# A two-layer hybrid encoder in one kernel: offsets between moving and next stationary operands changed

## The chip, the cores and the metric

The kernel runs on one core of a Trainium2 chip. The metric is device time in microseconds of one execution; the smaller the better. TensorE (PE) multiplies: each matmul has a stationary operand, loaded first by an instruction of its own (PEld), and a moving operand that streams past it; both lie in SBUF, the sums in PSUM. VectorE (DVE), ScalarE (ACT) and GpSimd (POOL) do the rest, and SyncE (SP) issues most transfers.

## The reference

Two pre-norm layers over 256 tokens of width 2048, each a token mixer with 4 cross-attention heads into 256 memory tokens beside it, an output projection, and a squared-ReLU MLP of width 8192. Layer 0's mixer is a neighbourhood attention with a bias per offset, layer 1's a grouped-query attention with normed heads and rotary positions.

```python
m = rms_norm(mem, mem_norm)
h = x
for i in range(DEPTH):
    n = rms_norm(h, attn_norm[i])
    ...
        z = n @ a_w_in[j]
        q, k, v, qm = jnp.split(z, [MIX_WIDTH, 2 * MIX_WIDTH, 3 * MIX_WIDTH], axis=-1)
        mix = neighbourhood_attention(split_heads(q, N_MIX_HEADS), split_heads(k, N_MIX_HEADS),
                                      split_heads(v, N_MIX_HEADS), a_rpb[j])
    ...
    km, vm = jnp.split(m @ w_mem_kv[i], 2, axis=-1)
    cross = memory_attention(split_heads(qm, N_MEM_HEADS), split_heads(km, N_MEM_HEADS),
                             split_heads(vm, N_MEM_HEADS))
    h = h + jnp.concatenate([mix, cross], axis=-1) @ w_o[i]
    n = rms_norm(h, mlp_norm[i])
    h = h + jnp.square(jax.nn.relu(n @ w_up[i])) @ w_down[i]
return rms_norm(h, final_norm)
```

## The kernel before

Every product is done in three matmuls of type float32r: an operand is split into a high part (ScalarE, L483: the name with `h`, as `hi`, `uh`, `bh`, `th`) and the rest (VectorE, L484: the name with `l`, as `lo`, `ul`, `bl`, `tl`), and high x high, high x low and low x high are summed in PSUM. Weights come from DRAM in chunks of 1 MB and are split half a chunk at a time.

There are two kinds of product. In an S product (`products`, L375, and its matmuls at L387) the weights are stationary and 256 tokens of an activation move, so a matmul has 256 columns; `k` counts the 16 slices (kt) of the inner dimension, and each has three matmuls: high weights with the activation's high part, high weights with its low part, low weights with its high part. In an M product (`m_products`, L355) the activations are stationary and 512 columns of weights move.

The stages in order: memory projections; layer 0's input projections and attention; its output projection; its MLP; the same for layer 1. In an MLP, 64 up chunks (`up_grains`, sum `ps_u`) give 128 features each. The first LEAD = 6 run alone. Then 58 steps follow (`STEPS`), each a part of the down product by Strassen's seven products (sums `p`, L1167 to L1170) around one up chunk: 12 matmuls on `bh`, `bl`; 48 of the up chunk; 9 on `th`, `tl`. That is 116 steps in both layers. The steps go in 8 runs a layer (`RUNS`), and at a run's end the seven sums are taken out of PSUM (`taken`). What Strassen leaves is done plainly (`plain_grains`, operands `h_p`, `l_p`, `uh`, `ul`); the last of these blocks, the closing block, is cut into 512 and twice 256 columns.

The order on each engine is decided by a scheduler when the program is built, from its own model of the times; `pin` and `issue_after` hold single instructions in place. Buffers go round by tag: `uh` and `ul` have two buffers each, so a split into one waits until PE has read its last use.

Tiles are placed in SBUF one behind the other by pool. The attention's pool (`work`) stands on the right side; the MLP's split weights are in `side` and `mlp`. Where an operand begins within 128 bytes is set by constants at the top, in bytes: MOVING_AT (weights that move, in a `uh` or `ul` buffer), LAST_AT (how far one half of the normed activation `hT` is set off in the last kt, class `Shifted`), LAST_COPY_AT (a copy `hT_l` of the last kt's first half, made at L1059 for the lead chunks and handed out by class `Plain`), U_AT and COPY_AT (the copy `u` of an up chunk's first stationary operand, made at L1049).

In an up chunk the last kt's three matmuls are, in order: high weights with the activation's second half, high weights with its first half, low weights with its first half (L381 and L382).

Of the kernel before, what the change touches and what calls it, by code (L numbers as in the profile page):

```python
# [46 lines left out]

MOVING_AT = 160

LAST_AT = 224  # L50

LAST_COPY_AT = 32

U_AT = 96

# [3 lines left out]

LONGER = {"hi": 128, "lo": 128}  # L60

COPY_AT = 384
MASKED = -1e30


# [12 lines left out]
class Work:  # L78


    def __init__(self, kind, src, acts, first, begins, last, start, done):
        self.kind, self.src, self.acts = kind, src, acts
        self.first, self.begins, self.last, self.start, self.done = first, begins, last, start, done
        self.early = self.behind = self.last_block = False


class Shifted:
# [5 lines left out]
    def __getitem__(self, key):  # L93
        _, k, s = key
        at = k * 512 + (s.start or 0)
        if k == KT - 1:

            at = k * 512 + (0 if s.start else SEQ + LAST_AT // 4)
        return self.room[:, at : at + SEQ]


class Plain:


    def __init__(self, shifted, last):
        self.shifted, self.last = shifted, last

    def __getitem__(self, key):
        _, k, s = key
        return self.shifted[key] if s.start or k < KT - 1 else self.last  # L110


class Near:
# [45 lines left out]
def encoder_kernel(ctx: ExitStack, tc: tile.TileContext, t: dict, out: bass.AP):  # L159
# [36 lines left out]

    def open_work():
        at.work = opened("work", side="right", bufs=2)

    open_sums(banks=2)  # L200
    open_ring()
# [173 lines left out]
    def products(ps, acts, k0, nk, hi, lo, keep_order=False, first=None):  # L375

        for j in range(nk):
            k = k0 + j
            s = slice(j * P, (j + 1) * P)
            parts = [(hi, slice(0, SEQ)), (hi, slice(SEQ, 512)), (lo, slice(0, SEQ))]  # L380
            if k == KT - 1:  # L381
                parts[:2] = parts[1::-1]  # L382
            elif j == 0 and isinstance(lo, Entered):
                parts = parts[2:] + parts[:2]
            for n, (x, part) in enumerate(parts):
                x = first if n == j == 0 and first is not None else x[:, s]
                ins = nc.tensor.matmul(ps, x, acts[:, k, part], start=k == n == 0,  # L387
                                       stop=k == KT - 1 and n == 2)
                if keep_order and n == 0:
                    pin(ins)  # L390
# [355 lines left out]
    def km_done(layer, hd):  # L746
        def f(w):
            if layer == 0:
                later((12, 12, 13, 8)[hd], put, w)
            else:  # L750
                put(w)

        def put(w):
            s = summed(w.ps, "km", box["mem_row"])
            if layer == 0:
                if hd == 0:
                    box["km"] = keys("km")
                split(box["km"][:, hd, :SEQ], box["km"][:, hd, SEQ:], s)
            else:
                k = at.work.tile([P, 512], F32R, tag="b_y2", name="km_w")  # L760
                split(k[:, :SEQ], k[:, SEQ:], s)
                nc.sync.dma_start(mem_k[:, hd, :], k.bitcast(F32))
        return f

    def vm_done(layer):
        def f(w):
            if layer == 0:
                box["vm"] = values("values", "vm", 1)
                put_values(box["vm"], w.ps, box["mem_col"])
                return  # L770
            for i in range(NT):
                v = at.work.tile([P, 2, 512], F32R, tag="pT", name="vm_w")
                put_value(v, w.ps[i], box["mem_col"][:, i : i + 1])
                nc.sync.dma_start(mem_v[:, i], v.bitcast(F32))
        return f

    def mem_back():

        box["km"] = keys("km")
        box["vm"] = values("values", "vm", 1)  # L780

        def load():

            with tc.issue_after(box["load"].ins):
                nc.sync.dma_start(box["km"].bitcast(F32), mem_k)
                for i in range(NT):
                    nc.sync.dma_start(box["vm"][:, :, i, :].bitcast(F32), mem_v[:, i])
        later(4, load)
# [231 lines left out]
    def up_grains(layer, m):  # L1020
        own = {}
        lead = m < LEAD

        def load():
            own["raw"] = loaded(t[f"w_up{layer}"][m], "U")

        def prep(hf):

            with tc.issue_after(box["summed"].ins) if m in (1, 2) else nullcontext():
                prepared(hf)  # L1030

        def prepared(hf):
            half = 2 * m + hf
            if lead and (half in (2, 4) or half > 4 and half % 3 == 2):

                if half < 5:
                    room = at.side.tile([P, 2, HALF], F32R, tag="b", bufs=2, name="u_b")
                    own[hf] = room[:, 0], room[:, 1]
                else:
                    s = slice(U_AT // 4, U_AT // 4 + HALF)  # L1040
                    own[hf] = tuple(at.mlp.tile([P, 3 * 512], F32R, tag=x, name=f"u_{x}")[:, s] for x in ("th", "tl"))
                box["splits"].append(split(*own[hf], own["raw"][:, hf * HALF : (hf + 1) * HALF]))
            else:
                own[hf] = half_of_side(own["raw"], hf)
            if not lead and hf == 0:

                room = at.side.tile([P, 256], F32R, tag="junk", bufs=1, name="u_0")
                own["first"] = room[:, COPY_AT // 4 :][:, :P]
                nc.scalar.activation(own["first"], own["raw"][:, :P], AF.Copy)  # L1049

        def run(hf):
            if m == hf == 0:
                closed("cat", "ring")
                at.mlp = opened("mlp")
                box["z"] = [at.mlp.tile([P, 4, 512], F32, tag=f"z{q}", name=f"z{q}") for q in range(2)]
                box["z_set"] = set()

                last = at.mlp.tile([P, 14 * P], F32R, tag="a", bufs=6, name="hT_l")[:, LAST_COPY_AT // 4 :][:, :SEQ]
                nc.scalar.activation(last, box["hT"][:, KT - 1, :SEQ].bitcast(F32), AF.Copy)  # L1059
                box["hT0"] = Plain(box["hT"], last)  # L1060
            if hf == 0:
                if lead:
                    own["ps"] = at.acc.tile([P, 512], F32, tag="acc", name="ps_u")[:, :SEQ]
                else:
                    own["ps"] = sum_of("up")[:, :SEQ]

            with tc.issue_after(box["late"].ins) if m == hf == 0 else nullcontext():
                products(own["ps"], box["hT0" if lead else "hT"], hf * (KT // 2), KT // 2, *own.pop(hf),
                         keep_order=not lead, first=own.pop("first", None))

        def after():
            squared(layer, m, own["ps"])

        soon = (8, 8, 3) if m == 1 else SOONER
        return [Grain(lambda: run(0), None, load, None, lambda: prep(0), soon),
                Grain(lambda: run(1), after, None, None, lambda: prep(1), SOONER)]

# [166 lines left out]
    def plain_grains(layer, nb, at_chunk):  # L1244
# [8 lines left out]

        def prep(c, hf):
            if (at_chunk + c) % 2 == 0:
                own[c, hf] = half_of_side(own[c], hf, MOVING_AT)
            else:
                own[c, hf] = tuple(at.mlp.tile([P, HALF], F32R, tag="bt"[hf] + x, name=f"{x}_p") for x in "hl")
                box["rest"] = split(*own[c, hf], own[c][:, hf * HALF : (hf + 1) * HALF])


# [152 lines left out]
    def rope_tables(name, c, factor=1.0):  # L1414

        cst = box["cst"]
        g = cst[:, c : c + HD]
        cg = at.work.tile([P, NT, HD], F32, tag="cos", bufs=1, name=f"cos_{name}")
        sg = at.work.tile([P, NT, HD], F32, tag="sin", bufs=1, name=f"sin_{name}")
        gs = g.rearrange("p (a b c) -> p a b c", a=2, b=2)  # L1420
        for i in range(NT):
            pin(nc.vector.scalar_tensor_tensor(cg[:, i, :], cst[:, C_COS + i * HD : C_COS + (i + 1) * HD], factor, g,
                                               op0=ALU.mult, op1=ALU.mult))
            s = cst[:, C_SIN + i * HD : C_SIN + (i + 1) * HD].rearrange("p (a b c) -> p a b c", a=2, b=2)
            d = sg[:, i, :].rearrange("p (a b c) -> p a b c", a=2, b=2)
            for b in range(2):
                pin(nc.vector.scalar_tensor_tensor(d[:, :, b, :], s[:, :, b, :], factor, gs[:, :, 1 - b, :],
                                                   op0=ALU.mult, op1=ALU.mult))
        box["rope"] = (cg, sg)
# [288 lines left out]
```

## Time and profile before

| | us |
|---|---|
| median of 3 runs | 2001.03 |
| lowest, highest of them | 1998.95, 2001.11 |
| profiled execution | 1999.8 |
| its span, first to last instruction | 1998.0 |

The mean granted TensorE clock over the span was 0.999 of full speed. The costliest groups of the page, by tile and engine:

| group | count | busy us | mean ns of one |
|---|---|---|---|
| PE L387, up chunks, high weights | 3812 | 663.0 | 276 |
| PE L387, up chunks, low weights | 1960 | 541.3 | 276 |
| ACT L483 `uh` | 262 | 277.7 | 1061 |
| DVE L484 `ul` | 262 | 318.3 | 1219 |
| DVE L484 `bl` | 116 | 265.2 | 2286 |
| DVE L484 `tl` | 116 | 203.5 | 1754 |

How to read the lines below: PE is the matmul, PEld its weight load. In a view of the timeline a line has the start in us from the span's start, the duration in us, the engine, the line, the operation, output<-inputs and shape, with x2 where two like instructions were merged; in brackets stands the engine's idle time before it and what ended that. A group's line ends with the count, busy us and mean ns of one, then the idle time before the group. A line of a stretch has its start and end, its length, and then busy us and count of PE, PEld, DVE, ACT and POOL, the granted clock, the share of DMA and GB/s. A matmul's duration is modelled and longer than the distance to the next one's start.

### The profile page before, as it was taken

Reading aid. Unit: us, or ns where it says so; the run is one execution under the profiler, and the core shown is the slowest. Engines: PE = TensorE matmul, PEld = TensorE weight load, DVE = VectorE, ACT = ScalarE, POOL = GpSimd, SP = SyncE. Lnnn points to the kernel's source line nnn. Section 1 sums busy time; section 2 is a strip of 40 time slices with the busy share of each in tenths; the row PEclk is TensorE's granted clock in tenths of the full one; section 3 lists DMA queues with packets and bytes.
Section 4 is the critical chain, followed back from the end, with each engine's and each line's share of the span. In section 5 each row is a group of like instructions: output and inputs, shape, how many; then the busy total and the mean of one; then the engine's idle time right before and its main releaser. Section 6 shows DMA issues by size and latency. Waiting matters only on the chain.

```text
span 1998.0 us, 32972 instructions
## 1 busy us (share of the span) xinstructions
PE 1985.7 (99%) x12872; PEld 1802.5 (90%) x12872; DVE 1722.1 (86%) x2164; ACT 1277.5 (64%) x1747; POOL 122.8 (6%) x169
## 2 busy tenths in 40 slices
PE   9999999999999999999999999999999999999998
PEld 8999999899999999999998888899999999999987
DVE  6777767589899999999999868779998999999997
ACT  6655555577676666666666666667666666666664
POOL 0000000000000000000000010000000000000000
PEclk9999999999999999999999999999999999999999
DMA  7856555757777777777667765557777777777763
GB/s 286 312 195 208 200 191 184 272 170 252 229 229 233 229 221 241 232 238 237 205 218 239 241 213 189 191 178 238 237 233 231 226 229 234 227 236 234 227 222 128
DMA packets 106862, 446.17 MB, mean 223 GB/s; under 512 B 18257, under 2 KB 39761, under 8 KB 59217
## 3 DMA queue, kind: packets, MB, share of 16 engines
q1 hardware_dynamic: 89712, 413.12, 58.6%
q0 software_dynamic: 16704, 30.42, 9.0%
q8 instruction: 101, 1.65, 0.3%
q10 hardware_dynamic: 288, 0.52, 0.1%
q14 instruction: 57, 0.46, 0.1%
HBM read 397.78 MB, written 4.19 MB: 201 GB/s over the span
## 4 chain that ended last, share of the span: by engine, by line
PE 95%; DVE 2%; DMA 1%; issue 1%; ACT 0%; SPq 0%; DVEq 0%; POOLq 0%; POOL 0%; ACTq 0%
PE ps_u L387 34%; PE ps_s L387 10%; PE p L1169 9%; PE p L1170 9%; PE p L1167 9%; PE ps_m L367 7%; PE ps_m L364 7%; PE ps_m L368 7%; DMA b<-b 0%; DVE lo L484 0%; DMA pT_t<-sc_t 0%; DMA first<-in_mem_rest 0%; DVE bl L484 0%; PE av L672 0%; PE av L673 0%
## 5 line engine op out<-in xcount | busy, mean ns | idle before, releaser
L387 PE MATMUL ps_u<-hT,uh 128*128 128x256 f32 x3812 | 663.0, 276 | 0.0
L387 PEld LDWEIGHTS ps_u<-hT,uh 128*128 128x128 f32 x3812 | 578.6, 188 | 5.5
L387 PE MATMUL ps_u<-hT,ul 128*128 128x256 f32 x1960 | 541.3, 276 | 0.0
L483 ACT ACTIVATE uh<-raw_U 128x1024 fp32r<-128x1024 f32 x262 | 277.7, 1061 | 234.3 <-PE ps_u L387 221.3
L387 PEld LDWEIGHTS ps_u<-hT,ul 128*128 128x128 f32 x1960 | 367.9, 188 | 0.0
L484 DVE TENSOR_TENSOR lo<-raw,hi 128x1024 fp32r<-128x1024 f32 (+1 forms) x215 | 254.7, 1191 | 110.0 <-ACT hi L483 108.9
L483 ACT ACTIVATE hi<-raw 128x1024 fp32r<-128x1024 f32 (+1 forms) x215 | 221.6, 1037 | 181.0 <-PE ps_m L368 93.2
L484 DVE TENSOR_TENSOR ul<-raw_U,uh 128x1024 fp32r<-128x1024 f32 x262 | 318.3, 1219 | 15.7 <-ACT uh L483 15.5
L483 ACT ACTIVATE bh<-b 128x2048 fp32r<-128x2048 f32 x116 | 222.9, 1921 | 104.7 <-PE p L1170 89.3
L484 DVE TENSOR_TENSOR bl<-b,bh 128x2048 fp32r<-128x2048 f32 x116 | 265.2, 2286 | 14.6 <-ACT bh L483 14.5
L484 DVE TENSOR_TENSOR tl<-t,th 128x1536 fp32r<-128x1536 f32 x116 | 203.5, 1754 | 37.7 <-ACT th L483 37.0
L483 ACT ACTIVATE th<-t 128x1536 fp32r<-128x1536 f32 x116 | 172.8, 1490 | 44.4 <-PE p L1170 40.9
L1169 PE MATMUL p<-bl,a_s 128*128 128x512 f32 x464 | 180.9, 390 | 1.8 <-DVE bl L484 1.6
L1170 PE MATMUL p<-bh,a_s 128*128 128x512 f32 x464 | 181.3, 391 | 0.0
L1167 PE MATMUL p<-bh,a_s 128*128 128x512 f32 x464 | 180.6, 389 | 0.0
L1139 POOL DMA_DIRECT2D b<-b x116 | 100.6, 867 | 1148.1 <-DVE t L1138 914.1
L387 PE MATMUL ps_s<-nT,hi 128*128 128x256 f32 x896 | 154.6, 277 | 0.0
L1167 PE MATMUL p<-th,a_s 128*128 128x512 f32 x348 | 136.1, 391 | 0.0
L1169 PE MATMUL p<-tl,a_s 128*128 128x512 f32 x348 | 135.8, 390 | 0.0
L387 PEld LDWEIGHTS ps_s<-nT,hi 128*128 128x128 f32 x896 | 135.3, 188 | 0.2
L1170 PE MATMUL p<-th,a_s 128*128 128x512 f32 x348 | 135.4, 389 | 0.0
L387 PE MATMUL ps_s<-nT,lo 128*128 128x256 f32 x448 | 124.2, 277 | 0.0
(304 smaller groups left out, 3500.1 us busy)
## 6 DMA issues: line engine op xcount, KB each, us to landing
raw_U<-in_w_up SPq DMA_DIRECT2D x128, 1024.0 KB, 4.9
b<-in_w_pair SPq DMA_DIRECT2D x116, 1024.0 KB, 4.9
raw<-in_w_o SPq DMA_DIRECT2D x32, 1024.0 KB, 4.9
b<-b POOLq DMA_DIRECT2D x116, 256.0 KB, 3.3
raw<-in_w_b SPq DMA_DIRECT2D x21, 1024.0 KB, 5.2
raw<-in_w_av SPq DMA_DIRECT2D x12, 1024.0 KB, 5.0
raw<-in_w_aq SPq DMA_DIRECT2D x12, 1024.0 KB, 4.9
raw<-in_w_ak SPq DMA_DIRECT2D x12, 1024.0 KB, 4.9
```

The source lines that it names most:

```text
L364: first = nc.tensor.matmul(ps, ah, hi[:, s], start=st, stop=False)
L367: nc.tensor.matmul(ps, ah, lo[:, s], start=False, stop=False)
L368: final = nc.tensor.matmul(ps, al, hi[:, s], start=False, stop=sp)
L387: ins = nc.tensor.matmul(ps, x, acts[:, k, part], start=k == n == 0, stop=k == KT - 1 and n == 2)
L483: first = nc.scalar.activation(dst_hi, src, AF.Copy)
L484: return first, nc.vector.tensor_tensor(dst_lo, src, dst_hi.bitcast(F32), op=ALU.subtract)
L1139: nc.gpsimd.dma_start(b[:, 3, :], b[:, 1, :], accum_op=ALU.add)
L1167: ins = nc.tensor.matmul(ps, a[:, 0, ai, :], hi[:, s], start=begins, stop=False)
L1169: nc.tensor.matmul(ps, a[:, 0, ai, :], lo[:, s], start=False, stop=False)
L1170: nc.tensor.matmul(ps, a[:, 1, ai, :], hi[:, s], start=False, stop=ends)
```

## The change

Offsets of operands change, by constants, by pads, and by an order:

- LAST_AT goes from 224 to 160, and `Shifted` sets off the second half of the last kt where it set off the first: with `s.start` set the operand lies at SEQ + LAST_AT // 4, else at 0, where before it was the other way round.
- In an up chunk (activations of class `Shifted`) the last kt's matmuls now run low weights first, then high weights with the first half, then high weights with the second half. For the other S products the order stays.
- The copy `hT_l`, the class `Plain` and LAST_COPY_AT go; the lead chunks read `hT` like the others.
- COPY_AT goes from 384 to 416.
- In the attention's pool, tiles of 64 bytes that nothing writes or reads (`apart`) are laid between keys, values, rotary tables and the rest: five places, three pads by name.
- In the closing block of layer 1 the moving weights are placed 64 bytes further on (MOVING_AT + 64 in `uh` and `ul`, and 16 elements on in `h_p` and `l_p`).

```diff
-LAST_AT = 224
-
-LAST_COPY_AT = 32
+LAST_AT = 160
...
-COPY_AT = 384
+COPY_AT = 416
...
         at = k * 512 + (s.start or 0)
         if k == KT - 1:
 
-            at = k * 512 + (0 if s.start else SEQ + LAST_AT // 4)
+            at = k * 512 + (SEQ + LAST_AT // 4 if s.start else 0)
         return self.room[:, at : at + SEQ]
...
-class Plain:
...
+    def apart(n):
+
+        at.work.tile([P, 16], F32, tag=f"apart{n}", bufs=1, name="apart")
...
             if k == KT - 1:
-                parts[:2] = parts[1::-1]
+                parts = parts[2:] + parts[:2] if isinstance(acts, Shifted) else [parts[n] for n in (1, 0, 2)]
...
             if layer == 0:
                 if hd == 0:
+                    apart(0)
                     box["km"] = keys("km")
                 split(box["km"][:, hd, :SEQ], box["km"][:, hd, SEQ:], s)
             else:
+                if hd == 0:
+                    apart(2)
                 k = at.work.tile([P, 512], F32R, tag="b_y2", name="km_w")
...
             if layer == 0:
+                apart(1)
                 box["vm"] = values("values", "vm", 1)
...
         box["km"] = keys("km")
+        apart(0)
         box["vm"] = values("values", "vm", 1)
...
-                last = at.mlp.tile([P, 14 * P], F32R, tag="a", bufs=6, name="hT_l")[:, LAST_COPY_AT // 4 :][:, :SEQ]
-                nc.scalar.activation(last, box["hT"][:, KT - 1, :SEQ].bitcast(F32), AF.Copy)
-                box["hT0"] = Plain(box["hT"], last)
...
-                products(own["ps"], box["hT0" if lead else "hT"], hf * (KT // 2), KT // 2, *own.pop(hf),
+                products(own["ps"], box["hT"], hf * (KT // 2), KT // 2, *own.pop(hf),
...
             if (at_chunk + c) % 2 == 0:
-                own[c, hf] = half_of_side(own[c], hf, MOVING_AT)
+                own[c, hf] = half_of_side(own[c], hf, MOVING_AT + 64 * last)
             else:
-                own[c, hf] = tuple(at.mlp.tile([P, HALF], F32R, tag="bt"[hf] + x, name=f"{x}_p") for x in "hl")
+                s = slice(16 * last, 16 * last + HALF)
+                own[c, hf] = tuple(at.mlp.tile([P, HALF + 16], F32R, tag="bt"[hf] + x, name=f"{x}_p")[:, s] for x in "hl")
...
         g = cst[:, c : c + HD]
+        if name == "k":
+            apart(1)
         cg = at.work.tile([P, NT, HD], F32, tag="cos", bufs=1, name=f"cos_{name}")
```

More of the change, by code (lines that the diff above doesn't have):

```diff
@@ L96, in __getitem__ @@
         if k == KT - 1:
-            at = k * 512 + (0 if s.start else SEQ + LAST_AT // 4)
+            at = k * 512 + (SEQ + LAST_AT // 4 if s.start else 0)
         return self.room[:, at : at + SEQ]
-class Plain:
[L105 to L110, printed above, removed]
 class Near:
```

## The prediction

> **What bounds the kernel now.** I read the page's busy shares, the chain of waits and the groups first, then stretches of the timeline.
>
> ```profile
> span 1998.0 us, 32972 instructions
> PE 1985.7 (99%) x12872; PEld 1802.5 (90%) x12872; DVE 1722.1 (86%) x2164; ACT 1277.5 (64%) x1747; POOL 122.8 (6%) x169
> PE 95%; DVE 2%; DMA 1%; issue 1%; ACT 0%; SPq 0%; DVEq 0%; POOLq 0%; POOL 0%; ACTq 0%
> L1169 PE MATMUL p<-bl,a_s 128*128 128x512 f32 x464 | 180.9, 390 | 1.8 <-DVE bl L484 1.6
> ```
>
> TensorE is the bound: the chain that ended last is 95% PE, and the largest wait of any PE group is 1.8 us. A busy PE is no proof, since a matmul's end is modelled (390 ns here, while they start 0.23 us apart). So the distance between starts is what I read, first with plain runs of matmuls.
>
> ```profile
> 1975.65 0.39 PE L364 MATMUL ps_m<-h_p,a_p 128*128 128x512 f32 x1
> ...
> 1983.81 0.28 PE L364 MATMUL ps_m<-uh,a_s 128*128 128x256 f32 x1
> ...
> 1989.45 0.28 PE L368 MATMUL ps_m<-h_p,a_p 128*128 128x256 f32 x1
> ```
>
> From 1975.65 there are 36 matmuls of 512 columns: 8.16 / 36 = 226.7 ns each. From 1983.81 to 1989.45 lie 47 steps of 256 columns: 5.64 / 47 = **120.0 ns**. Now the same shape in an up chunk, and in layer 1's attention.
>
> ```profile
> 804.01 0.40 PE L1170 MATMUL p<-bh,a_s 128*128 128x512 f32 x1
> 804.25 0.28 PE L387 MATMUL ps_u<-hT,u 128*128 128x256 f32 x1
> 804.36 0.28 PE L387 MATMUL ps_u<-hT,uh 128*128 128x256 f32 x1
> ...
> 809.58 0.28 PE L387 MATMUL ps_u<-hT,ul 128*128 128x256 f32 x1
> 809.70 0.40 PE L1167 MATMUL p<-th,a_s 128*128 128x512 f32 x1
> ```
>
> ```profile
> 1195.85 0.28 PE L579 MATMUL sc_ps<-kT,qT 128*128 128x256 f32 x1
> 1195.97 0.28 PE L580 MATMUL sc_ps<-kT,qT 128*128 128x256 f32 x1
> 1196.09 0.28 PE L579 MATMUL sc_ps<-kT,qT 128*128 128x256 f32 x1
> 1196.20 0.28 PE L580 MATMUL sc_ps<-kT,qT 128*128 128x256 f32 x1
> ...
> 1198.60 0.28 PE L581 MATMUL sc_ps<-kT,qT 128*128 128x256 f32 x1
> ```
>
> Up chunk: 46 steps from 804.36 to 809.58, 5.22 / 46 = **113.5 ns**. Attention: 24 matmuls, 23 steps, 2.75 / 23 = **119.6 ns**. Same engine, shape and type, no wait in any of the three, yet 6 ns apart. In the two built programs I took, for each matmul, the SBUF address of its moving operand less that of the next matmul's stationary one, modulo 128 bytes. In the up chunk it is 64. In the two slow runs it is 0. That offset is what the change sets, so the question is how many pairs move and whether PE's time is still the bound afterwards.
>
> **The change part by part.** Both programs issue 12858 matmuls, PE's order differing only where the last kt of an up chunk is turned. Pairs whose offset moves, counted over the programs:
>
> 256 columns, 0 to 64: 366 (203 in the attentions, 116 at the last matmul of an up chunk before the Strassen part, 47 in the closing block). 256 columns, 32 to 64: 118, nearly all inside the last kt of an up chunk. 512 columns, 32 to 0: 116, the last bh before an up chunk's first stationary `u` (COPY_AT). 320 and 160 columns, 0 to 64: 48 and 24, layer 0's near attention. 512 columns, 0 to 64: 24, and 32 to 96: 31. 256 columns, 32 to 96: 23, and 64 to 96: 10.
>
> *Attention, 203 pairs.* The long run gives 119.6 - 113.5 = 6.1 ns. The first pairs of a run are cheaper (1196.09 to 1196.20 is 0.11), and most attention runs are short, so I take 5.7: 203 x 5.7 = **1.2 us** (0.8 at 4 ns, 1.3 at 6.5).
>
> *Closing block, 47 pairs* (MOVING_AT + 64 and the shifted odd tiles): 47 x (120.0 - 113.5) = **0.3 us**.
>
> *The 116 Strassen steps, three pairs each.* Two rows of the chain of waits, 26 steps apart, give the step.
>
> ```profile
> 456.70 5.45 PE ps_u L387 x48
> ...
> 722.60 5.45 PE ps_u L387 x48
> ```
>
> (722.60 - 456.70) / 26 = 10.227 us. A step is 48 matmuls of 256 and 21 of 512: 48 x 0.1134 + 21 x 0.2267 = 10.204 at the plain distances (0.1134 lies within the rounding of 5.22 / 46). So at most some 20 ns a step can come back. The bh before `u` starts at 804.01 and `u` at 804.25, 0.24 where plain pairs are 0.227: 8 ns with the rounding. The chunk's last pair, 809.58 to 809.70, is 0.12 against 0.1134: 5 ns. The third lies between rows; I take 4, less than the 6 of an offset of 0. 17 ns x 116 = **2.0 us**, between 0.9 (the first pair alone) and 2.3 (20 ns).
>
> *Near attention, 72 pairs.*
>
> ```profile
> 161.77 0.31 PE L558 MATMUL sc_ps<-kT,qT 128*128 128x320 f32 x1
> 161.91 0.24 PE L560 MATMUL sc_ps<-kT,qT 128*128 128x160 f32 x1
> 161.99 0.35 PE L558 MATMUL sc_ps<-kT,qT 128*128 128x320 f32 x1
> 162.17 0.24 PE L560 MATMUL sc_ps<-kT,qT 128*128 128x160 f32 x1
> 162.25 0.32 PE L387 MATMUL ps_s<-nT,lo 128*128 128x256 f32 x1
> 162.40 0.40 PE L387 MATMUL ps_s<-nT,hi 128*128 128x256 f32 x2
> ```
>
> The first 320 takes 0.14, the second 0.18, and the 256 behind the second 160 takes 0.15: the matmul after a short one is held by its own weight load, 0.08 being too short to cover it. There an offset may give nothing. Between -0.1 and 72 x 6 = 0.43 us; I take **0.2**.
>
> *Pairs no row shows at their new offset* (512 columns at 64 or 96, 55 of them): the nearest rows differ by 8 ns, so 55 x 8 = 0.44 us either way; I take 0, since the sign is unknown. The 10 pairs that go from 64 to 96 lose about 4 ns each, 0.04 us.
>
> *The copy that goes.*
>
> ```profile
> L1059 ACT ACTIVATE hT_l<-hT x2: 419/420/421, 427.6 to 1334.8; 128x256 fp32r<-128x256 f32 x2
> ```
>
> Two copies of 0.42 us, with PE busy throughout on the lead chunks and reading the copy only at each chunk's last kt: nothing on the path. The pads add no instruction.
>
> *What the turned kt does to ACT.* The last reader of a `uh` buffer is now the chunk's last matmul, so the buffer comes free together with the sum, and in the built program the ReLU (L1085) stands ahead of the next `uh` split instead of behind it, in almost every step.
>
> ```profile
> 799.55 1.06 ACT L483 ACTIVATE uh<-raw_U 128x1024 fp32r<-128x1024 f32 x1 [1.66 <-PE ps_u L387]
> 800.52 0.37 ACT L1085 ACTIVATE c<-ps_u 128x256 f32<-128x256 f32 x1
> 801.72 1.49 ACT L483 ACTIVATE th<-t 128x1536 fp32r<-128x1536 f32 x1 [0.38 <-PE p L1170]
> ```
>
> ```profile
> 800.65 1.23 DVE L484 TENSOR_TENSOR ul<-raw_U,uh 128x1024 fp32r<-128x1024 f32 x1 [0.44 <-ACT uh L483]
> 801.79 0.81 DVE L1096 TENSOR_TENSOR c<-c 128x128 f32<-128x128 f32 x3
> 803.24 1.76 DVE L484 TENSOR_TENSOR tl<-t,th 128x1536 fp32r<-128x1536 f32 x1 [0.64 <-ACT th L483]
> ```
>
> `uh` would start one matmul (0.11) and one ReLU (about 0.35) later, 0.45 us. Behind it wait `ul` on VectorE, then `c` and `tl`. In this step DVE already idles 0.64 before `tl`, because `th` waits for PE at 801.72 and not for ACT; the 0.45 comes out of that idle time. This `ul` is the second half of the next chunk, which PE reaches 24 matmuls after 804.25, at about 807.0; it would end at about 802.3, so PE sees nothing. Cost taken: 0; it is the slower rival's entry if DVE has no such idle time.
>
> **Sum**: 1.2 + 0.3 + 2.0 + 0.2 - 0.04 = **3.6 us**, between 1.5 (0.8 + 0.3 + 0.9 - 0.1 - 0.44) and 4.8 (1.3 + 0.3 + 2.3 + 0.43 + 0.44). The profiled execution took 1999.8 us (its span and 1.8 around it), so 1996.2 by it. The three runs shown (1998.95, 2001.03, 2001.11) have a median 1.2 above it; the mean of all four is 2000.2, which I use: **1996.6**.
>
> **The rivals.** *VectorE takes the MLP part back.* DVE's share in the MLPs:
>
> ```profile
> 700.00:900.00 200.00, 200.00 (x1354) 183.75 (x1353) 186.31 (x203) 134.25 (x147) 16.67 (x20) 1.00 0.73 231
> 1880.00:1925.00 45.00, 44.34 (x294) 39.85 (x292) 42.08 (x52) 27.14 (x32) 3.44 (x4) 1.00 0.69 215
> ```
>
> ```profile
> 1924.05 0.39 PE L1167 MATMUL p<-bh,a_s 128*128 128x512 f32 x1
> 1926.01 0.50 PE L1169 MATMUL p<-bl,a_s 128*128 128x512 f32 x1 [1.57 <-DVE bl L484]
> ```
>
> At 1924 PE does stand still for `bl`, 1.96 us between two starts. If DVE set the MLPs' pace, their 2.0 us would stay: 2000.2 - 1.6 = 1998.6. Against it: 186.31 of 200 us leave DVE 13.69 / (200 / 10.227) = 0.70 us idle a step, and 0.02 is wanted of it. For it: around run changes (the second window) the slack is gone.
>
> *Slower: the ReLU ahead of `uh`.* If DVE, at the 16 run ends where it also adds the partial sums, cannot swallow the 0.45 us, PE waits there for `ul` or `bl`: up to 16 x 0.45 = 7.2, less 3.6 gained, 2003.8. It decides from the point where DVE's idle 0.70 a step is below the added wait. Against it: where DVE is behind, `uh` has been waiting for it, so a later `uh` costs nothing.
>
> *The offset does nothing.* The three runs also differ in which operand moves (activations or split weights) and how it is laid out; if that makes the 6 ns, the time stays 2000.2. The Trainium skill speaks for this one: "TensorE: Matmul & The Clock Gate", section "Step-by-step: what each phase is for", says PE reads SBUF through two independent ports, so that loading the next weights takes nothing from the running matmul. By that rule no address pair can matter and the change gives 0; the runs at 113.5 and 120.0 ns, both without a wait, do not fit one fixed distance, but only the new kernel separates address from layout.
>
> *More than summed*: the 0 to 64 pairs of 512 and the near attention all gain, 4.8 us, 1995.4.
>
> **How the numbers follow.** Forecast 62%, VectorE 11%, slower 9%, nothing 8%, more 10%. A measurement of this kernel can tell about 0.2% from no change, 4.0 us, so the border lies at 1997.0. The forecast's centre is 0.4 under it, and runs shown scatter by 1 us either way: two thirds of the forecast and all of "more" count as faster, 0.41 + 0.10, and 0.03 by the scatter of the other cases, **0.54**. Slower by over 0.2% needs more than the slower rival's price, **0.06**; the rest, **0.40**, is within. The forecast's own range is 1995.4 to 1998.7; the range to hold 8 of 10 takes in scatter and part of "nothing": 1994.5 to 2000.5.
>
> **What would show it.** Right: 256-column runs in the attention and the closing block at 113 to 114 ns a start; a step of 10.21 us instead of 10.227; bh to `u` at 0.227; ReLU ahead of `uh` on ACT, DVE's wait before `ul` longer and before `tl` shorter. Wrong: those runs still at 119 to 120 (layout, not address); steps of 10.21 but new waits of PE for `bl` or `ul` (VectorE, or the ReLU); the 1.96 us at 1924 grown by more than the MLP gained.

## The result, and the profile after

The changed kernel takes **2002.66 us** (median of 22 runs, 2001.59 to 2005.80), the kernel before 2000.22 beside it (22 runs, 1998.48 to 2003.66). The medians lie 2.4 us apart; the ratio is 1.0014 with a 95% interval of 1.0008 to 1.0020, so the change costs between 1.6 and 4.0 us. The forecast was 1996.6 with a range of 1994.5 to 2000.5: a gain was forecast and a loss was measured, and the time lies outside the range.

The first lines of the page after, its shares of the chain, and one row of its groups:

```profile
span 2001.9 us, 32911 instructions
PE 1988.3 (99%) x12872; PEld 1805.3 (90%) x12872; DVE 1724.7 (86%) x2164; ACT 1262.9 (63%) x1745; POOL 125.2 (6%) x169
PE 94%; DVE 2%; DMA 2%; issue 1%; ACT 1%; SPq 0%; DVEq 0%; POOLq 0%; POOL 0%; ACTq 0%
L1161 PE MATMUL p<-bl,a_s 128*128 128x512 f32 x464 | 181.0, 390 | 2.8 <-DVE bl L475 2.6
```

TensorE has the same 12872 matmuls and is busy 2.6 us longer. So matmuls do not wait, for the most part: they start further apart. The chain of waits groups a run of matmuls into one row (start, length, what, number). Here are two kinds of run that the prediction did not look at, before and then after:

```profile
162.41 10.93 PE ps_s L387 x96
...
424.09 29.83 PE ps_u L387 x263
1331.44 29.83 PE ps_u L387 x263
```

```profile
161.68 11.34 PE ps_s L378 x96
...
425.17 30.34 PE ps_u L378 x263
1333.53 30.34 PE ps_u L378 x263
```

The first is a stretch of layer 0's projection between two blocks of near attention: 10.93 / 96 = 113.9 ns a matmul before, 11.34 / 96 = **118.1** after. The change moves none of its operands. The second is the lead up chunks, in both layers: 113.4 before, 115.4 after, 0.51 us a layer by these rows (0.47 from start to start), and five of the 263 pairs have a new offset.

Now the places that the prediction named, in the timeline after. Attention, then the closing block:

```profile
1197.34 0.28 PE L570 MATMUL sc_ps<-kT,qT 128*128 128x256 f32 x1
...
1200.10 0.29 PE L572 MATMUL sc_ps<-kT,qT 128*128 128x256 f32 x1
...
1979.58 0.39 PE L355 MATMUL ps_m<-h_p,a_p 128*128 128x512 f32 x1
...
1987.81 0.28 PE L355 MATMUL ps_m<-uh,a_s 128*128 128x256 f32 x1
...
1993.35 0.28 PE L359 MATMUL ps_m<-h_p,a_p 128*128 128x256 f32 x1
```

Attention: 2.76 / 23 = 120.0 ns, where it was 119.6. Closing block: the 512s take 8.23 / 36 = 228.6 (were 226.7), the 256s 5.54 / 47 = 117.9 (were 120.0). And the step, by the chain of waits, 26 steps apart:

```profile
458.25 5.45 PE ps_u L378 x48
...
724.14 5.45 PE ps_u L378 x48
```

(724.14 - 458.25) / 26 = 10.227 us, what it was. Inside a step the timeline after shows why:

```profile
805.56 0.39 PE L1162 MATMUL p<-bh,a_s 128*128 128x512 f32 x1
805.79 0.28 PE L378 MATMUL ps_u<-hT,u 128*128 128x256 f32 x1
805.91 0.28 PE L378 MATMUL ps_u<-hT,uh 128*128 128x256 f32 x1
806.02 0.28 PE L378 MATMUL ps_u<-hT,ul 128*128 128x256 f32 x1
```

bh to `u` is 0.23 as forecast (was 0.24), but `u` to `uh` is now 0.12 and not 0.11. As a mean over the 116 steps, bh to `u` goes from 235.0 to 226.7 ns, 8.3 less, and the next three distances from 112.5 to 117.5, from 113.3 to 115.8 and from 113.3 to 114.1, 8.3 more. **The gain is given back by the matmuls right behind it.** The turned last kt does the same: its two pairs gain 4.2 and 1.7 ns, and the second and third matmul of 512 columns behind them pay 1.7 and 4.2 back.

Since both programs run the same matmuls in the same order of shapes, each start can be set against the same matmul's start in the first trace of before, and the difference read stage by stage. Microseconds more than that trace, one execution each (e1 to e8 are the experiments below, the two "again" are second executions of the same programs; "wait" is a place where TensorE stands still for an operand):

| kernel | up to 95 us | layer 0 to 360 us | lead chunks, 2 layers | MLP steps | layer 1 attention | wait at 1236 | wait at 1588 | wait at 1924 | closing |
|---|---|---|---|---|---|---|---|---|---|
| before again | -1.32 | 0.00 | 0.00 | -0.04 | 0.00 | 0.20 | 0.63 | 0.04 | 0.01 |
| after | -0.88 | **1.96** | **0.93** | 0.01 | 0.00 | 0.56 | 1.49 | -0.13 | -0.03 |
| after again | 0.11 | **1.96** | **0.93** | -0.03 | 0.03 | -0.23 | 0.00 | 0.00 | 0.00 |
| e1 | -1.42 | **1.96** | 0.00 | -0.03 | 0.02 | 0.05 | 1.22 | -0.55 | 0.00 |
| e2 | -0.57 | 0.00 | **0.93** | 0.00 | -0.01 | 0.54 | 3.99 | -0.68 | 0.00 |
| e3 | -1.05 | 0.00 | -0.01 | -0.01 | -0.01 | 0.03 | 0.00 | -0.03 | -0.01 |
| e4 | -0.63 | 0.05 | 0.00 | -0.03 | 0.01 | 0.21 | 0.00 | 0.26 | -0.02 |
| e5 | -0.27 | **1.96** | **0.93** | -0.03 | 0.01 | 0.39 | 0.00 | 1.93 | -0.05 |
| e6 | -0.45 | **1.96** | -0.01 | -0.03 | 0.00 | 0.36 | 0.00 | 0.40 | -0.03 |
| e7 | -1.29 | **2.51** | 0.00 | -0.02 | 0.04 | 0.05 | 0.00 | 0.30 | 0.01 |
| e8 | -1.09 | **2.51** | -0.01 | -0.03 | 0.04 | 0.49 | 1.12 | 1.88 | 0.14 |

Two columns belong to the program: 1.96 and 0.93 us come back in both executions of the changed kernel. Their sum, 2.9 us, lies within the measured 1.6 to 4.0. Four columns (the first and the three waits) differ between two executions of one program. The pairs can be told apart too, by the addresses in the two built programs: those whose offset the change moves come out 1.5 us shorter in all, and the sum of the program's columns, 2.9, leaves 4.4 us more on pairs that it does not move.

### The profile page after: what moved, and what is told of

The parts are those of the page before. It is cut to its first block, busy times and chain, and to the rows that moved or that the text cites. A ratio compares the mean times of both kernels' runs of the same rounds, so it can differ in the third digit from the quotient of the medians.

```text
span 2001.9 us, 32911 instructions
## 1 busy us (share of the span) xinstructions
PE 1988.3 (99%) x12872; PEld 1805.3 (90%) x12872; DVE 1724.7 (86%) x2164; ACT 1262.9 (63%) x1745; POOL 125.2 (6%) x169
## 4 chain that ended last, share of the span: by engine, by line
PE 94%; DVE 2%; DMA 2%; issue 1%; ACT 1%; SPq 0%; DVEq 0%; POOLq 0%; POOL 0%; ACTq 0%
PE ps_u L378 34%; PE ps_s L378 10%; PE p L1161 9%; PE p L1162 9%; PE p L1159 9%; PE ps_m L358 7%; PE ps_m L359 7%; PE ps_m L355 7%; DMA b<-b 1%; DVE bl L475 0%; DVE lo L475 0%; DMA pT_t<-sc_t 0%; DMA raw<-in_w_first 0%; DMA h_r<-h_b 0%; PE av L665 0%
## 5 line engine op out<-in xcount | busy, mean ns | idle before, releaser
L378 PE MATMUL ps_u<-hT,uh 128*128 128x256 f32 x3820 | 670.2, 276 | 0.0
L378 PE MATMUL ps_u<-hT,ul 128*128 128x256 f32 x1968 | 523.2, 276 | 0.0
L378 PEld LDWEIGHTS ps_u<-hT,ul 128*128 128x128 f32 x1968 | 360.3, 188 | 0.0
L475 DVE TENSOR_TENSOR lo<-raw,hi 128x1024 fp32r<-128x1024 f32 (+1 forms) x215 | 254.8, 1190 | 112.5 <-ACT hi L474 111.3
L1077 ACT ACTIVATE c<-ps_u 128x256 f32<-128x256 f32 x128 | 49.0, 383 | 187.3 <-PE ps_u L378 187.3
```

Of the source, the lines that this page charges most:

```text
L475: return first, nc.vector.tensor_tensor(dst_lo, src, dst_hi.bitcast(F32), op=ALU.subtract)
L1077: nc.scalar.activation(two, ps, AF.Relu)
```

## The experiments

The theories, as the expectations call them. **A**: the prediction's; the offset modulo 128 sets each pair's distance by itself. **B**: TensorE's starts go in a rhythm; at the same addresses there is a fast one (113.4 ns for 256 columns) and a slow one (117.8), and what came before decides which holds until something else breaks it. **C**: another engine's traffic makes the slow one. **D**: the waits for `bl` hang on when a load lands.

**m1: matmuls alone.** The kernel's core, with `m` and `s` the two offsets in bytes (a pair is written (m, s) from here on: where the moving operand starts, and where the next stationary one does, modulo 128; both lie in one piece here):

```
a = (i % 4) * 512 + m // 4
b = (i % 16) * 128 + s // 4
nc.tensor.matmul(ps[bank][:, :n], sta[:, b : b + P], mov[:, a : a + n], start=begin, stop=end)
```

> This kernel computes none of the reference: it runs matmuls alone on one core, with no other engine at work, in runs of 36 with one pair of start offsets (moving operand at 0, 32, 64 or 96, next stationary operand at 0, 32, 64 or 96, modulo 128 bytes), each run twice: once behind six 512-column matmuls and once behind four short ones (320, 160, 320, 160 columns) of the near attention's shape. It then repeats the pair (0, 64) behind such short ones at sixteen other pairs of offsets. Theory A (the prediction's): the distance between starts hangs on the difference of the two offsets alone, 113.4 ns at 64 (all four such pairs, (64, 0) and (96, 32) too), 120 at 0, 117.5 at 32 and 96, and is the same behind either entry. Theory B (rhythm): the same pair of addresses has two steady distances, about 113.4 and 117.8 ns, and what came before the run decides which; some entries give 117.8 for 30 matmuls on end at (0, 64). Theory C (a third party on the way to SBUF makes the 117.8 in the big kernel): every (0, 64) run here is at 113.4, since no other engine works.

Measured, steady distances of 256 columns in ns (moving offset down, stationary across; first behind 512s, then behind short matmuls):

| | 0 | 32 | 64 | 96 |
|---|---|---|---|---|
| 0 | 120.0, 120.0 | 118.4, 118.4 | **117.8, 113.4** | 117.5, 117.2 |
| 32 | 116.7, 116.7 | 120.0, 120.0 | 118.4, 118.4 | 113.4, 113.4 |
| 64 | 113.4, 113.4 | 116.7, 116.7 | 120.0, 120.0 | 118.3, 118.3 |
| 96 | 120.2, 119.9 | **117.8, 113.3** | 117.7, 117.7 | 120.0, 120.0 |

Half of A stands, for operands in one piece: a difference of 0 is always 120.0, and only 64 reaches 113.4. But 64 apart is not enough: (0, 64) and (96, 32) go at 117.8 or 113.4 by what stood ahead of the run, for all of its 36 matmuls. Behind blocks of short matmuls at the sixteen pairs of offsets, 13 of 32 runs at (0, 64) or (32, 96) were slow from end to end. For 512 columns a difference of **0** is best, 226.7; 64 gives 228.8 or 233.4. C falls: the slow rhythm is there with no other engine at work.

**e1, e2, e3: the change in parts.** e1 is the kernel before with the `apart` pads alone. e2 has the last kt alone:

```
-LAST_AT = 224
+LAST_AT = 160
...
-            at = k * 512 + (0 if s.start else SEQ + LAST_AT // 4)
+            at = k * 512 + (SEQ + LAST_AT // 4 if s.start else 0)
...
-                parts[:2] = parts[1::-1]
+                parts = parts[2:] + parts[:2] if isinstance(acts, Shifted) else [parts[n] for n in (1, 0, 2)]
```

with the `hT_l` copy taken out. e3 has COPY_AT = 416 and the two lines of the closing block.

> The kernel before with the attention's pads alone. Theory A (64 apart gives 113.4 ns, pair by pair): 203 attention pairs and 72 near ones faster, 1.4 us less, 1998.8 against 2000.2. Theory B (rhythm carried over): layer 1's attention no faster (118 to 120 ns), and in layer 0 the projections' runs between near-attention blocks go from 113.4 to 117.8 ns, though their own addresses stay, so that 1.9 us more have come by 340 us and the time is 2002.1; the MLP step stays at 10.227 us.

> The kernel before with the turned last kt alone (with its LAST_AT and without the copy). Theory A: 9 ns a step, 1.0 us less, 1999.2. Theory B: in an MLP step the gain at the chunk's last two pairs (about 6 ns) comes back at the next chunk's first ones, the step stays within 4 ns of 10.227, and the lead chunks lose 0.4 to 0.5 us a layer, so about 2001.1. Rival (ReLU ahead of uh on ScalarE costs time): beside that TensorE stands still for bl at about 1588 us (1.4 us) and for lo at about 1236 us (0.6 us), 2003.1; if the 1.4 us were chance, it is not there again.

> The kernel before with COPY_AT 416 and the closing block's shift alone, which lie in different stages of one trace. Theory A: 8 ns a step (0.9 us) and 0.3 us in the closing block, 1999.0. Theory B: bh to u goes from 235 to 227 ns and the next two matmuls lose 5 and 2 ns, so the step gains 0 to 1 ns; the closing block gains 0.1 us (pairs of 256 at 118 ns instead of 120); 2000.1.

Measured: e1 2001.24, e2 2000.18, e3 1999.85 against 1999.74 (ratios 1.0009, 1.0003, 1.0003; intervals 1.0000 to 1.0018 and twice 0.9994 to 1.0012). The times alone tell little; the chain of e1 and of e2 tells it:

```profile
161.14 11.34 PE ps_s L391 x96
...
424.63 29.83 PE ps_u L391 x263
```

```profile
161.84 10.93 PE ps_s L385 x96
...
423.52 30.34 PE ps_u L385 x263
```

The pads make the 1.96 us, the last kt the 0.93; the third part does nothing at all. A falls three times. B holds in layer 0, in the lead chunks and in the step, but not everywhere: its 0.1 us in e3's closing block did not come (0.00), e2's gain at the last kt comes back in the 512s right behind and not at the next chunk's first matmuls, and its times for e1 and e2, 2002.1 and 2001.1, were 0.9 us too long. In e3 the step's three distances change as in the changed kernel, by 8, 5 and 3 ns, and the MLPs' 116 steps come out 0.01 us apart: the return is exact. The wait of e2 at 1588 us is dealt with under e5.

**e4: the same pads, 128 bytes long** (layer 0's two, none in layer 1):

```
-        at.work.tile([P, 16], F32, tag=f"apart{n}", bufs=1, name="apart")
+        at.work.tile([P, 32], F32, tag=f"apart{n}", bufs=1, name="apart")
```

> The kernel before with layer 0's two pads made 128 bytes long instead of 64, and no pad in layer 1: the operands move by 128 or 256 bytes and every start stays what it was modulo 128. Theory B (the offsets modulo 128 of the short matmuls decide in which rhythm the following run goes): the runs between the near attention's blocks stay at 113.4 ns as before, nothing of the 1.9 us is there by 340 us, and the time is that of before, 1999.7 to 2000.2. Rival (any other place of the tiles does it, a bank or a collision with another engine's writes): some runs at 117.8 ns, 0.5 to 2 us more.

Measured: 1999.12 against 2000.98 (ratio 0.9994, 0.9985 to 1.0004). Its chain:

```profile
161.84 10.93 PE ps_s L391 x96
```

10.93 again. So a move by 128 or 256 bytes does nothing, and one that changes the start modulo 128 does. B's number stands, to 0.05 us.

**m2: MLP steps and attention blocks alone.**

> This kernel computes none of the reference: matmuls alone, no other engine at work. First MLP steps of 48 matmuls of 256 columns and 21 of 512, at sixteen sets of offsets (the 512s with both operands at 0, 32, 64 or 96; the 256s with moving and stationary at (32, 96), (0, 64), (64, 0) or (96, 32)), five steps each; then twenty matmuls at (0, 64) between near-attention blocks of 320, 160, 320, 160 columns at sixteen pairs of offsets; then runs of 24 behind 13 of 512 columns. Theory A (each pair's distance by its own offset): all sixteen steps take 10.200 us (48 x 113.33 + 21 x 226.67), and the runs of 24 with 64 between all go at 113.4. Theory B (rhythm): the change from one width to the other costs some 15 to 40 ns a time, so a step takes 10.22 to 10.28 us; where a 256 run never comes into the fast rhythm, 48 x 4.4 = 0.21 us more; of the sixteen attention offsets about a third leave the run behind them at 117.8, and of the runs of 24 those at (0, 64) and (96, 32) too.

Measured: repeated steps took 10.246 to 10.473 us, none 10.200. Where the 256s came into the fast rhythm, 10.246 to 10.300; where not, 10.41 to 10.47. With the 512s at (32, 32) and the 256s at (0, 64), five steps in a row took 10.246, 10.247, 10.247, **10.473**, 10.247 us: the same 69 matmuls, 0.23 us apart. Between attention blocks at (32, 0), three times the same 24 matmuls took 2.875, 2.785 and 2.877 us. Seven of 48 such runs were slow, fewer than the third that B had expected. Runs of 24 behind 512s: 119.7 ns at (96, 96), 114.7 at (32, 96), 117.8 to 117.9 at the other three pairs with 64 between. The kernel's 10.227 us is shorter than any of these steps.

**e5: `uh` ahead of the ReLU again**, in the changed kernel:

```
-            squared(layer, m, own["ps"])
+            if lead or m >= UPS - 2:
+                squared(layer, m, own["ps"])
+            else:
+                later(2, squared, layer, m, own["ps"])
```

> The changed kernel with each chunk's ReLU and Square issued one grain later, which puts uh ahead of the ReLU again in 114 steps, as before. Rival of the prediction (the ReLU ahead of uh makes bl late at 1588 us): the stall of 1.4 us there is gone and so are some of the 2.4 us that the changed kernel lost, 2001.2. Theory D (that stall hangs on when the load of b lands, which took 5.9, 6.9, 7.6, 7.7 and 8.0 us in five traces, with a stall from the third on): the stall may be there or not, the step is 10.228 us either way, layer 0 loses 1.9 us and the lead chunks 0.9 us as in the changed kernel; 2002.0 to 2002.7.

Measured: 2002.87 against 2000.98 (ratio 1.0012, 1.0003 to 1.0020): nothing of the loss comes back. The wait at 1588 us is gone in this execution, but it is gone in "after again" too, where the ReLU is still ahead of `uh`; it is there in e1 and in "before again", where the ReLU never was ahead. So the order on ScalarE is not its cause. In the chain of the first trace after, what leads to that wait is a DMA:

```profile
1576.94 8.93 DMA b<-b
...
1585.95 1.93 ACT bh L474
1587.88 0.03 issue
1587.90 2.30 DVE bl L475
```

The load of `b` ahead of it, in the list of DMA issues between 1572 and 1577 us, of e3, before, and e2 in turn (the last number is us from issue to landing):

```profile
b<-in_w_pair SPq DMA_DIRECT2D x1, 1024.0 KB, 5.9
```

```profile
b<-in_w_pair SPq DMA_DIRECT2D x1, 1024.0 KB, 6.9
```

```profile
b<-in_w_pair SPq DMA_DIRECT2D x1, 1024.0 KB, 8.0
```

With 5.9 and 6.9 there is no wait, with 8.0 the longest (e2's profiled execution, which loses 4 us there; eight of its eleven executions are 3.5 to 4.6 us shorter). All twelve traces go this way: no wait with loads of 5.2 to 7.1 us, starts 0.7 us or more apart with the five of 7.5 to 8.0. D fits, though why the load takes longer in one execution is not shown.

**e6: a copy for the lead chunks' far half**, in the changed kernel, so that no pair of theirs is (64, 96), called an odd pair below:

```
+        return self.last if s.start and k == KT - 1 else self.shifted[key]
...
+                last = at.mlp.tile([P, 14 * P], F32R, tag="a", bufs=6, name="hT_l")[:, 8:][:, :SEQ]
+                nc.scalar.activation(last, box["hT"][:, KT - 1, SEQ:512].bitcast(F32), AF.Copy)
+                box["hT0"] = Plain(box["hT"], last)
```

> The changed kernel in which the lead chunks read the far half of the last kt from a copy that starts at 32 modulo 128, so that their five pairs of (64, 96) in each layer become (32, 96); all else as changed. The prediction priced those ten pairs at 4 ns each, 0.04 us. Theory B: in the changed kernel each of them turns the rhythm of the 48 matmuls behind it from 113.4 to 117.8 ns or back, so without them the 0.455 us at 424 to 447 us and the 0.445 us at 1330 to 1375 us are gone, while layer 0 keeps its 1.9 us: 0.9 us less than changed, 2001.8 against 2002.7 (in the trace: up chunks of the lead at 113.4 throughout). Rival (the lead chunks are slower for another reason, the order of the last kt itself): the 0.9 us stay.

Measured: 2002.02 against 1999.12 (ratio 1.0013, 1.0004 to 1.0022). The timeline of the changed kernel, then of e6, behind the second chunk's odd pair:

```profile
431.37 0.39 PE L378 MATMUL ps_u<-hT,uh 128*128 128x256 f32 x2
...
438.80 0.39 PE L378 MATMUL ps_u<-hT,uh 128*128 128x256 f32 x2
```

```profile
431.81 0.39 PE L389 MATMUL ps_u<-hT,uh 128*128 128x256 f32 x2
...
438.95 0.39 PE L389 MATMUL ps_u<-hT,uh 128*128 128x256 f32 x2
```

7.43 us against 7.14 for the same 63 distances: 117.9 and 113.3 ns. One matmul at (64, 96) puts those behind it into the slow rhythm, though these stand at (32, 96) as before; a second odd pair, 13 matmuls on, leaves them there, and a third, 48 further, puts them back. With the copy, 0.93 us are gone to within 0.01: B's number. The total does not show it, since its scatter is as large.

**e7, e8: the moving operands moved instead.** With the change's pads and one more of 64 bytes behind `pT_t` in the pool, the attention's pairs are (32, 96) instead of (96, 32). e7 is the kernel before with all these pads, e8 the changed kernel with the further pad and e6's copy:

```
+            apart(3)
```

> The kernel before with pads that move the attention's moving operands by 64 bytes (from 96 to 32) and leave the stationary ones at 96, modulo 128: pairs at (32, 96) instead of the change's (96, 32). Theory A: as good as the change's pads, 1.4 us less. Theory B (by the matmuls run alone: behind short matmuls at (32, 96) a (0, 64) run stays at 113.4 and the block is 7 ns shorter than at (96, 96); a run of 24 behind 512 columns goes from 119.7 to 114.7 ns): layer 0's runs stay at 113.4, -0.2 to +0.1 us by 340 us; the run of 24 at about 1196 us takes 0.1 us less; short runs in layer 1 gain another 0 to 0.4 us; in all 0.1 to 0.6 us less than before.

> The changed kernel with both repairs: the lead's copy, and the moving instead of the stationary operands moved by 64 bytes in the attention. Theory B: layer 0 and the lead chunks lose nothing any more, the MLP step stays at 10.228 us, so the time is that of before or up to 0.5 us under it, 1999.5 to 2000.2 against 2000.0; what stands in the trace beyond that is TensorE's wait for bl or lo where a load lands late. Theory A: 3.6 us less than before.

Measured: 2002.33 and 2002.35 against 1999.12 (both ratios 1.0018, 1.0009 to 1.0027). Both expectations failed. The chain of e7:

```profile
161.04 11.34 PE ps_s L398 x96
```

The run is slow again, and layer 0 loses 2.51 us instead of 1.96. The two rhythms are there, but which of them an entry leads to could not be carried over from matmuls alone to the kernel. Layer 1's run of 24, for which 0.1 us less was expected, did not get shorter either (see below). No version was faster than the kernel before by more than the noise.

**The same two programs again.**

> The kernel before once more, for what differs between two executions of one program. Theory B (the rhythm follows from the program alone): all runs between 95 and 340 us at 113.4 ns, the stage from 95 to 360 us within 0.1 us of the first trace, the lead chunks at 113.4 ns, the step 10.228 us. Theory D (the waits for bl hang on when a load lands): the first 37 us differ by up to 1.4 us and the waits at 1588 and 1924 us by up to 1 us from the first trace, though the program is the same.

> The changed kernel once more. Theory B: 1.9 us more than the kernel before between 95 and 360 us, 0.455 and 0.445 us more in the lead chunks, matmul for matmul as in the first trace of the changed kernel. Theory D: the wait for bl at 1588 us (1.3 us more than before in the first trace) is another one, 0 to 2.3 us; the wait for lo at 1236 us, 0.56 us in the first trace, is seen to repeat or not.

Measured: 1999.30 and 2002.68, one run each. Layer 0 and the lead chunks repeat to within 0.01 us. The wait at 1588 us does not:

```profile
1585.02 0.39 PE L1167 MATMUL p<-bh,a_s 128*128 128x512 f32 x1
1585.72 0.50 PE L1169 MATMUL p<-bl,a_s 128*128 128x512 f32 x1 [0.32 <-DVE bl L484]
```

```profile
1588.94 0.39 PE L1159 MATMUL p<-bh,a_s 128*128 128x512 f32 x1
1589.16 0.39 PE L1161 MATMUL p<-bl,a_s 128*128 128x512 f32 x1
```

The kernel before waits here this time (0.70 between starts), and the changed kernel does not (0.22).

## Why the prediction was wrong

**The step that failed** is the one from two plain runs to a rule: "That offset is what the change sets", with the distance between starts a property of each pair, so that pairs could be counted and multiplied. The reading of the bound was right (TensorE, by the distance between starts), the offsets moved as counted, and 113.5 and 120.0 are true steady distances. What was taken for a price per pair is, in the long runs, the pace of a rhythm that a run falls into and keeps; in the steps, a gain that the matmuls behind give back; and in one of the two slow runs something that the pair does not set at all.

- *Attention, 1.2 us*: 0.1, summed over the 203 pairs in the first trace after. The long run went from 119.6 to 120.0 ns at its new pair (96, 32), which m1 shows at 117.8 or 113.3. In e7 it stands at (32, 96), the pair of the up chunk's 113.5, for which m1's table has 113.4:

```profile
1197.14 0.28 PE L590 MATMUL sc_ps<-kT,qT 128*128 128x256 f32 x1
...
1199.07 0.28 PE L590 MATMUL sc_ps<-kT,qT 128*128 128x256 f32 x1
...
1199.91 0.29 PE L592 MATMUL sc_ps<-kT,qT 128*128 128x256 f32 x1
```

The whole run takes 2.77 / 23 = 120.4 ns a start and its last seven distances 0.84 / 7 = 120.0. At three pairs of offsets, (96, 96), (96, 32) and (32, 96), it settles at 120.0, so for this run the prediction's own sign of "layout, not address" came. The moving operand is not in one piece: class `Far` hands out 8 pieces of 32 columns, 512 bytes apart. The 62 of the 203 pairs that have it did not change in the mean; the other 141 gained 0.8 ns each, not 5.7. That the pieces are the reason is likely but not shown, since m1 and m2 move operands in one piece.
- *Near attention, 0.2 us, and what lies between its blocks*: cost 1.96 us. The runs of 256 between the blocks were not in the sum, since none of their pairs moved. e1 shows that they pay, e4 that the starts modulo 128 of what the pads move decide it; that the short matmuls right ahead do it is read from their place.
- *The ten pairs from 64 to 96, 0.04 us*: 0.93 us, e2 and e6. Each sets the pace of the matmuls up to the next odd pair. Here the copy that was called free to drop had kept the pairs at 32.
- *The 116 steps, 2.0 us*: 0.0. The distances forecast at bh to `u` came (235 to 227); the return in the next matmuls was not looked for. The row that was quoted, 10.227 us against a plain 10.204, was read as 20 ns to be had; m2 has no step under 10.246.
- *Closing block, 0.3 us*: 0.03. The 256s gained 2 ns, the 512s lost 2: the prediction had set the 512s at a new offset to 0 for want of a row.
- *ScalarE's order, 0 us*: right, and as forecast. ScalarE and VectorE after:

```profile
801.22 0.38 ACT L1077 ACTIVATE c<-ps_u 128x256 f32<-128x256 f32 x1 [1.77 <-PE ps_u L378]
801.50 1.05 ACT L474 ACTIVATE uh<-raw_U 128x1024 fp32r<-128x1024 f32 x1
```

```profile
802.58 1.22 DVE L475 TENSOR_TENSOR ul<-raw_U,uh 128x1024 fp32r<-128x1024 f32 x1 [0.83 <-ACT uh L474]
803.72 0.81 DVE L1088 TENSOR_TENSOR c<-c 128x128 f32<-128x128 f32 x3
804.79 1.76 DVE L475 TENSOR_TENSOR tl<-t,th 128x1536 fp32r<-128x1536 f32 x1 [0.26 <-ACT th L474]
```

The ReLU stands first; the wait ahead of `ul` grew from 0.44 to 0.83, and that ahead of `tl` shrank from 0.64 to 0.26. The slower rival named this order and got the sign of the result right for a reason that e5 takes away.

- *VectorE takes the MLP part back*: not what happened, though the step is unchanged as that rival says. The return is made within two matmuls, with no wait of TensorE.
- *The offset does nothing*: not for operands in one piece, by m1, but it is what the attention's long run shows. The Trainium skill ("TensorE: Matmul & The Clock Gate", section "Step-by-step: what each phase is for") says that the two read ports are independent, so that loading the next weights takes nothing from the running matmul. m1 does not agree: with nothing else at work, 120.0 and 113.4 ns differ by the two start addresses alone.

Open: the waits at 1236 us (from 0.23 less to 0.56 more) and 1588 us were seen to differ between executions, not why; what holds the attention's run at 120.0 ns; and what picks the rhythm.

## What to carry to other kernels

A difference between two steady runs is not a price per instruction: before it is multiplied by a count, look at the distances right behind an odd pair in the same trace, and at long runs downstream of what moves, even where their own operands stay. Compare runs whose operands are laid out alike: a row's `128x256` does not tell one piece from eight. Set two traces against each other matmul by matmul and by stage; it showed differences of 0.01 us where the times of 11 runs had an interval of some 2 us either way. When a second execution of the same program differs in a wait, that wait is no evidence on a change.

## What was not expected of the hardware

**Two paces at one set of addresses.** The fast one costs the same per column as the best 512s (113.3 / 256 = 226.7 / 512 = 0.443 ns). The slow one adds 4.4 ns a matmul and held for up to 95 matmuls in a row in the kernel. The program alone does not always pick it: m1 and m2 open with the same 400 matmuls at (0, 64), of which, behind the first, 18 distances in m1 and 25 in m2 are 213 ns, and from then on m1 goes at 117.8 and m2 at 113.3 to the end of the run.

**A half clock behind a wait.** In e2 TensorE's starts at 1588 us lie 2.33 us apart, and then:

```profile
1591.12 0.63 PE L1161 MATMUL p<-bh,a_s 128*128 128x512 f32 x1
1591.55 0.63 PE L1163 MATMUL p<-bl,a_s 128*128 128x512 f32 x1
1591.98 0.63 PE L1164 MATMUL p<-bh,a_s 128*128 128x512 f32 x1
```

Starts are 0.43 apart where 0.23 is usual, and the granted clock of the stretch (last but two in its row of windows) is 0.62:

```profile
1589.60:1593.00 3.40, 3.40 (x10) 2.67 (x11) 3.40 (x5) 1.38 (x2) 0.00 (x0) 0.62 0.63 236
```

With that the stage loses 3.99 us in the table, where the wait itself grew by 2.1. The half rate came again at 1924 us in e5 and e8, behind 2.30 and 2.20 us, and did not come behind 2.24, 2.33 and 2.26 us in e4, e6 and e7: the length alone does not decide. The Trainium skill (same page, section "What's actually happening") has the clock at half rate after an idle window of about 3.4 us that runs free of the program. The half rate agrees, and a free window could be why like waits differ, which no run here shows; gaps of 2.20 to 2.33 us between starts, shorter than 3.4, were enough here.
